# Where the operands of the main matrix products lie in SBUF, modulo 256 bytes

## The chip, the cores and the metric

The kernel runs on one core of a Trainium2 chip. The metric is the device time of one execution in microseconds; the time before is the median of three runs. TensorE (PE) multiplies, VectorE (DVE) and ScalarE (ACT) work element by element, GpSimd (POOL) and SyncE (SP) mostly start transfers here. SBUF is the on-chip memory from which all of them read: 128 partitions, each a row of bytes, and an address below is a byte address within a partition.

## What is computed

One layer of a decoder trunk on 288 tokens (256 of a prompt, 32 of eight short samples), in float32. A short convolution mixer and a gated delta-rule mixer share one input projection; their outputs are merged, and a feed-forward block follows:

```python
proj = x @ w_in                                   # 2048 -> 11280 columns
y_a = (gB * conv_out) @ w_a_out
y_b = o.reshape(Bsz, L, D_GDN).astype(x.dtype) @ w_b_out
merged = sigmoid(m_a) * y_a + sigmoid(m_b) * y_b
x = layer_norm(ALPHA * x + merged @ w_o, ln1_g, ln1_b)
hid = square(relu(x @ w_up))                      # 2048 -> 8192
x = layer_norm(ALPHA * x + hid @ w_down, ln2_g, ln2_b)
```

## The kernel before

**Tiling.** Every large product is computed transposed: the features of the result lie on the partitions and the 288 tokens run along the row. A block of weights is four slices of 128 input rows by 256 output columns (512 KB), and a group of blocks makes 256 columns of the result in two banks of PSUM. The table `blocks` lists all of them in the order in which they run: the input projection with the delta rule woven between its matmuls, the merge (sigmoid gates from `w_in`, each with its product with `w_a_out` or `w_b_out`), the product with `w_o`, and four times a quarter of `w_up` (eight groups) followed by a quarter of `w_down` (eight groups; the last of them has its final group turned round, L747).

**High and low parts.** Float32 precision is put together from three products of a rounded type. Each operand is split into a high part, rounded by ScalarE (`split_hi`, L184), and a low part, the remainder, made by VectorE (`split_lo`, L139 as its helper). For every slice k of 128 rows and both halves of 128 columns, `matmuls` issues the three products high x high, high weights x low activations, and low weights x high activations, so six matmuls to a slice, in this order: xh with the first half of `hi`, xl with the same half, xh and xl with the second half, then xh with the first half of `lo` and with its second half. In the profile these are lines L216 (with `hi`) and L218 (with `lo`). Each matmul has its own load of 128 x 128 weights.

**Names.** The activations are `xh` and `xl` in the projection and for the gates, `ahl` and `ohl` (high and low halves in one tile) for the products with `w_a_out` and `w_b_out`, `mh` and `ml` for `w_o`, `dh` and `dl` for `w_up`, and `hh` and `hl` for `w_down`. `hh` and `hl` take over the memory of `xh` and `xl` (the pool's tags XH and XL), and the others share four regions, R1 to R4. A tag names one piece of memory which several tiles use in turn.

**Loads and lead.** `load` starts the transfer of a block seven blocks ahead, and the two splits follow three blocks ahead of the matmuls, in four buffers each for `raw`, `hi` and `lo`. The order of instructions on each engine is written out by hand; no scheduler moves anything. What places the tiles in memory is the order in which pools and tags are first asked for, and their sizes.

**Places.** A row of `hi` or `lo` is 1024 bytes to a slice and 512 to a half, so all weights of one kind lie at one place modulo 256. One slice of activations is 288 tokens, 1152 bytes (four and a half times 256), so that the places of successive slices alternate by 128. `dh` and `dl` hold 290 columns a slice (NX, with two columns for the layer norm's gain and offset, which only the first quarter of `w_up` uses), 1160 bytes, so their place moves on by 136 with each slice; `ohl` has this pitch too. `w_o`'s evacuation `wo_evac` writes `dh` and `dl` for the first quarter, and `normal` overwrites them, 288 columns wide, for the other three. `acc` is the running sum of the feed-forward block.

The lines that walk through the activations:

```python
for k in range(kb):
    xh_, xl_ = ah[:, k0 + k, 0:n], al[:, k0 + k, 0:n]
    ...
    for o, c, x in both[::2] + both[1::2] if i == 0 else both:
        pe.matmul(o, h[:, k, c], x, start=st and x is xh_, stop=False)
    for o, c in ts:
        pe.matmul(o, l[:, k, c], xh_, start=False, stop=en)
```

Of the kernel before, what the change touches and what calls it, by code (L numbers as in the profile page):

```python
# [9 lines left out]
F32 = mybir.dt.float32  # L10
# [6 lines left out]
P = 128  # L17
# [4 lines left out]
NX = NT + 2  # L22
# [79 lines left out]
def hybrid_kernel(ctx: ExitStack, tc: tile.TileContext, A):  # L102
# [141 lines left out]
    ones = cst("ones")  # L244

    xh = xp.tile([P, KT, NT], F32R, tag="XH", name="xh")
    xl = xp.tile([P, KT, NT], F32R, tag="XL", name="xl")
    hw = cp.tile([P, 24, 28], F32, name="hw")
    hwa = cp.tile([P, 8, 19], F32, name="hwa")
# [155 lines left out]
    def yb_evac(p):  # L405
        def f(ps):
            if p == 0:
                ph["mh"] = ph["pool"].tile([P, KT, NT], F32R, tag="R1", name="mh")
                ph["ml"] = ph["pool"].tile([P, KT, NT], F32R, tag="R2", name="ml")
            s = slice(2 * p, 2 * p + 2)  # L410
            t = ph["pool"].tile([P, 2, NT], F32, tag="yt", name=nm("yt"), bufs=2)
            tt(t, ps[:, :, 0:NT], ph["sg"], MUL)
            tt(t, t, ph["mg"][:, s, :], ADD)
            act.copy(ph["mh"][:, s, :], t)
            tt(ph["ml"][:, s, :], t, ph["mh"][:, s, :], SUB)
        return [f]
# [4 lines left out]
    for p in range(8):  # L421
        add_group(w_in, C_MB + GW * p, 0, KT, acts_x, [sig_evac])
        add_group(A["w_b_out"][0], GW * p, 0, 8, lambda: (ph["oh"], ph["ol"]), yb_evac(p))

    def wo_evac(p):
        q = slice(2 * p, 2 * p + 2)

        def resid(ps):
            pl = ph["pool"]
            if p == 0:  # L430
                ph["dl"] = pl.tile([P, KT, NX], F32R, tag="R3", name="dl")
                ph["dh"] = pl.tile([P, KT, NX], F32R, tag="R4", name="dh")
                t = ap_.tile([P, 2, H, NT], F32, tag="ao", name="lns").rearrange("p a h t -> p (a h) t")
                ph["qa"], ph["da"], ph["c"] = t[:, 0:2], t[:, 2:4], t[:, 4]
                ph["ln"] = [t[:, 5 + u] for u in range(4)]
                dh, dl = ph["dh"], ph["dl"]
                gbc = lnp[:, 0:32].rearrange("p (a k) -> p k a", a=2)
                act.copy(hmr, ones)
                act.copy(dh[:, :, NT:NX], gbc)
                tt(dl[:, :, NT:NX], gbc, dh[:, :, NT:NX], SUB)  # L440
            ph["s"] = pl.tile([P, 2, NT], F32, tag="yt", name=nm("s"), bufs=2)
            dd = ph["s"]
            stt(dd, xh[:, q, :], ALPHA, ps[:, :, 0:NT], MUL, ADD)
            stt(dd, xl[:, q, :], ALPHA, dd, MUL, ADD)
            if p:
                tt(dd, dd, bmid(ph["c"], 2), SUB)

        def centre(ps):
            tt(ph["c"], ph["s"][:, 0, :], ph["s"][:, 1, :], ADD)
            ph["chl"] = high_low(ph["c"], "sg")  # L450

        def shift(ps):
            cps = gtile()
            dd = ph["s"]
            row_sums(cps[:, 0:NT], ph["chl"])
            act.mul(ph["c"], cps[:, 0:NT], 1.0 / 256)
            tt(dd, dd, bmid(ph["c"], 2), SUB)

        def scaled(ps):
            dd, qa, da = ph["s"], ph["qa"], ph["da"]  # L460
            sd = ph["pool"].tile([P, 2, NT], F32, tag="sg", name=nm("sd"), bufs=2)
            for u in range(2):
                k = 2 * p + u
                dve.tensor_scalar(out=sd[:, u, :], in0=dd[:, u, :], scalar1=lnp[:, k:k + 1], scalar2=None, op0=MUL)
            act.copy(ph["dh"][:, q, 0:NT], sd)
            tt(ph["dl"][:, q, 0:NT], sd, ph["dh"][:, q, 0:NT], SUB)

        def sums(ps):
            dd, qa, da = ph["s"], ph["qa"], ph["da"]
            if p == 0:  # L470
                act.activation(qa, dd, AF.Square)
                act.copy(da, dd)
            else:
                s2 = ph["pool"].tile([P, 2, NT], F32, tag="sg", name=nm("sq"), bufs=2)
                act.activation(s2, dd, AF.Square)
                tt(da, da, dd, ADD)
                tt(qa, qa, s2, ADD)

        def both(*fs):
            def f(ps):  # L480
                for g in fs:
                    g(ps)
            return f

        if p == 0:
            return [resid, centre, lambda ps: None, shift, both(scaled, sums)]
        if p < 7:
            return [resid, both(scaled, sums)]
        return [both(resid, scaled, sums), halve, lambda ps: None, lambda ps: None, norms]
# [17 lines left out]
    def norms(ps):  # L507
        s1, s2 = gtile(), gtile()
        for t, u in ((s1, "dahl"), (s2, "qahl")):
            row_sums(t[:, 0:NT], ph[u])  # L510
        dm, va, av, nb = ph["ln"]
        act.mul(dm, s1[:, 0:NT], INV_D)
        tt(va, dm, dm, MUL)
        stt(va, s2[:, 0:NT], INV_D, va, MUL, SUB)
        act.activation(va, va, AF.Sqrt, bias=epsc[:, 0:1])
        dve.reciprocal(out=av, in_=va)
        stt(nb, dm, -1.0, av, MUL, MUL)
        ph["acc"] = ph["pool"].tile([P, KT, NT], F32, tag="R1", name="acc")


    def normal(p):
# [18 lines left out]
            act.mul(ph["acc"][:, q, :], t, ALPHA)  # L540

        def f3():
            t, h = tl["t"], ph["dh"][:, q, 0:NT]
            act.copy(h, t)
            tt(ph["dl"][:, q, 0:NT], t, h, SUB)
        return f, f2, f3

    for p in range(8):
# [317 lines left out]
    mark["up"] = len(blocks)  # L866
    for c in range(4):
        for p in range(8):
            add_group(A["w_up"][0], 2048 * c + GW * p, 0, KT, lambda: (ph["dh"], ph["dl"]), up_evac(c, p),
                      NT if c else NX)  # L870
        mark["down", c] = len(blocks)
        if c == 3:
            mark["down3"] = len(blocks)
        acts_h = lambda: (ph["hh"], ph["hl"])
        for p in range(8 if c < 3 else 7):
            add_group(A["w_down"][0], GW * p, 2048 * c, KT, acts_h, down_evac(c, p))
# [755 lines left out]
    steps = x_steps(0, 1)  # L1632
    t0, o0 = steps[0]()
    his[0] = wp.tile([P, KB, GW], F32R, tag="hi", name=nm("hi"))
    los[0] = wp.tile([P, KB, GW], F32R, tag="lo", name=nm("lo"))
    t, h0, l0 = raw.pop(0), his[0], los[0]

# [45 lines left out]
    for i in range(len(blocks)):  # L1683
# [50 lines left out]
        if i == mark["merge"]:  # L1734
            gcm.__exit__(None, None, None)
            p3 = pool("p3")
            ph["pool"] = p3
            r1 = p3.tile([P, KT, NT], F32R, tag="R1", name="ahl")
            r4 = p3.tile([P, KT, NX], F32R, tag="R4", name="ohl")
            ph["mg"] = p3.tile([P, KT, NX], F32, tag="R3", name="mg")[:, :, 0:NT]  # L1740

            def halves(key, r, src):
                for q in range(2):
                    s = slice(4 * q, 4 * q + 4)
                    s8 = slice(8 + 4 * q, 12 + 4 * q)
                    act.copy(r[:, s, 0:NT], src[:, s, :])
                    tt(r[:, s8, 0:NT], src[:, s, :], r[:, s, 0:NT], SUB)
                ph[key + "h"], ph[key + "l"] = r[:, 0:8, :], r[:, 8:16, :]

            halves("a", r1, gd["ao"][:, 0])  # L1750
            at(i + 9, lambda: halves("o", r4, gd["ao"][:, 1]))
# [58 lines left out]
```

## Time and profile before

| what | value |
|---|---|
| median of 3 runs (lowest to highest) | 1650.71 us (1650.47 to 1650.87) |
| span of the profiled execution | 1648.8 us |
| matmuls of TensorE, all | 12857 |
| of these, three-product matmuls 288 or 290 columns wide (L216, L218) | 11808 |
| busy PE, DVE, ACT, POOL | 1641.3, 986.9, 780.0, 137.0 us |

The span runs from the first to the last instruction, and the device time holds some 2 us more. PE's busy time is no measure of how well it runs, since matmuls are pipelined and their ends are modelled. What can be read is how far apart the starts of successive matmuls stand, or, in a long stretch without a wait, its length over the number of matmuls in it.

The ends of the stages, as the times at which the first matmul on new activations starts: merge 424.07 us, `w_o` 717.39 us, the quarters of `w_up` 819.64, 1024.83, 1229.04 and 1433.25 us, those of `w_down` 922.86, 1127.07, 1331.28 and 1535.49 us, the last group 1627.45 us.

### The profile page before, as it was taken

What the parts mean: (1) busy time and instruction counts of PE and PEld (TensorE: products, weight loads), DVE (VectorE), ACT (ScalarE), POOL (GpSimd) and SP (SyncE); (2) the same over time, 40 slices, a digit from 0 to 9 for tenths busy, and PEclk for the clock granted to TensorE, in tenths of its full rate; (3) what the DMA queues carried; (4) which work ended last, traced back from release to release, by engine and by line L of the source; (5) the groups of instructions that cost most, each with busy time, mean ns of one, the idle gap of its engine ahead of it and who ended that gap; (6) DMA issues with size and microseconds to landing.
All of it is one profiled execution on the core that took longest, in us unless ns stands there. A gap on an engine that the chain in (4) does not pass through costs nothing.

```text
span 1648.8 us, 30931 instructions
## 1 busy us (share of the span) xinstructions
PE 1641.3 (100%) x12857; PEld 1628.9 (99%) x12857; DVE 986.9 (60%) x1342; ACT 780.0 (47%) x1215; POOL 137.0 (8%) x286
## 2 busy tenths in 40 slices
PE   9999999999999999999999999999999999999998
PEld 8999999999999999999999999999999999999998
DVE  6787788878544444457776666444444444444466
ACT  7774678367533333334354454443334433344454
POOL 1232214234000000000000000000000000000111
PEclk9999999999999999999999999999999999999999
DMA  8567466846655555555565555555555555555652
GB/s 267 176 174 207 141 173 198 226 116 187 189 167 166 166 166 167 167 167 160 177 202 166 167 166 167 166 165 165 165 164 164 165 166 166 167 166 167 181 164 100
DMA packets 278999, 282.49 MB, mean 171 GB/s; under 512 B 15075, under 2 KB 272920, under 8 KB 278596
## 3 DMA queue, kind: packets, MB, share of 16 engines
q1 hardware_dynamic: 274394, 268.42, 54.7%
q0 software_dynamic: 4032, 11.63, 2.5%
q8 instruction: 101, 1.65, 0.4%
q10 hardware_dynamic: 432, 0.46, 0.1%
q14 instruction: 40, 0.33, 0.1%
HBM read 272.83 MB, written 7.63 MB: 170 GB/s over the span
## 4 chain that ended last, share of the span: by engine, by line
PE 98%; ACT 0%; DVE 0%; POOL 0%; issue 0%; ACTq 0%
PE acc L216 63%; PE acc L218 31%; PE acc L747 1%; PE g L1538 0%; PE g L1558 0%; PE g L1561 0%; PE g L1338 0%; PE g L1238 0%; PE g L1511 0%; PE g L1550 0%; PE g L1347 0%; PE g L1042 0%; PE g L701 0%; PE g L1422 0%; PE g L1399 0%; DVE lo L139 0%
## 5 line engine op out<-in xcount | busy, mean ns | idle before, releaser
L139 DVE TENSOR_TENSOR lo<-raw,hi 128x1024 fp32r<-128x1024 f32 (+1 forms) x503 | 606.7, 1210 | 560.0 <-ACT hi L184 558.5
L184 ACT CAST hi<-raw 128x1024 fp32r<-128x1024 f32 (+1 forms) x499 | 518.8, 1042 | 724.9 <-PE acc L216 630.2
L216 PE MATMUL acc<-xh,hi 128*128 128x288 f32 x1408 | 397.3, 298 | 1.0 <-ACT xh L956 1.0
L216 PE MATMUL acc<-xl,hi 128*128 128x288 f32 x1408 | 393.8, 295 | 0.0
L218 PE MATMUL acc<-xh,lo 128*128 128x288 f32 x1408 | 302.0, 295 | 0.1
L216 PE MATMUL acc<-dl,hi 128*128 128x288 f32 (+1 forms) x1024 | 287.7, 295 | 0.0
L216 PE MATMUL acc<-dh,hi 128*128 128x288 f32 (+1 forms) x1024 | 287.4, 295 | 0.0
L216 PE MATMUL acc<-hl,hi 128*128 128x288 f32 x992 | 277.8, 295 | 0.0
L216 PE MATMUL acc<-hh,hi 128*128 128x288 f32 x992 | 277.4, 294 | 0.0
L216 PEld LDWEIGHTS acc<-xh,hi 128*128 128x128 f32 x1408 | 264.3, 188 | 3.4 <-ACT xh L956 1.5
L216 PEld LDWEIGHTS acc<-xl,hi 128*128 128x128 f32 x1408 | 264.2, 188 | 0.6
L218 PEld LDWEIGHTS acc<-xh,lo 128*128 128x128 f32 x1408 | 225.9, 188 | 0.4 <-DVE lo L139 0.3
L218 PE MATMUL acc<-dh,lo 128*128 128x288 f32 (+1 forms) x1024 | 219.8, 296 | 0.0
L218 PE MATMUL acc<-hh,lo 128*128 128x288 f32 x992 | 213.2, 296 | 0.0
L216 PEld LDWEIGHTS acc<-dh,hi 128*128 128x128 f32 x1024 | 193.3, 189 | 0.0
L216 PEld LDWEIGHTS acc<-dl,hi 128*128 128x128 f32 x1024 | 192.8, 188 | 0.0
L216 PEld LDWEIGHTS acc<-hh,hi 128*128 128x128 f32 x992 | 186.4, 188 | 0.4 <-issue 0.4
L216 PEld LDWEIGHTS acc<-hl,hi 128*128 128x128 f32 x992 | 186.1, 188 | 0.0
L218 PEld LDWEIGHTS acc<-dh,lo 128*128 128x128 f32 x1024 | 164.6, 188 | 0.0
L218 PEld LDWEIGHTS acc<-hh,lo 128*128 128x128 f32 x992 | 159.0, 188 | 0.0
L216 PE MATMUL acc<-mh,hi 128*128 128x288 f32 x256 | 71.9, 297 | 0.0
L216 PE MATMUL acc<-ml,hi 128*128 128x288 f32 x256 | 71.7, 295 | 0.0
(424 smaller groups left out, 1475.0 us busy)
## 6 DMA issues: line engine op xcount, KB each, us to landing
raw<-in_w_in_dram SPq DMA_DIRECT2D x175, 512.0 KB, 3.8
raw<-in_w_up_dram SPq DMA_DIRECT2D x128, 512.0 KB, 3.8
raw<-in_w_down_dram SPq DMA_DIRECT2D x128, 512.0 KB, 3.6
raw<-in_w_o_dram SPq DMA_DIRECT2D x32, 512.0 KB, 3.5
raw<-in_w_a_out_dram SPq DMA_DIRECT2D x16, 512.0 KB, 3.7
raw<-in_w_b_out_dram SPq DMA_DIRECT2D x16, 512.0 KB, 3.5
out_dram<-S POOLq DMA_DIRECT2D x8, 512.0 KB, 4.5
S<-in_state_gdn_dram POOLq DMA_DIRECT2D x4, 512.0 KB, 6.4
```

Of the source, the lines that this page charges most:

```text
L139: dve.tensor_tensor(out=out, in0=a, in1=b, op=op)
L184: act.copy(his[i][:, k:k + step], raw[i][:, k:k + step])
L216: pe.matmul(o, h[:, k, c], x, start=st and x is xh_, stop=False)
L218: pe.matmul(o, l[:, k, c], xh_, start=False, stop=en)
L747: pe.matmul(out, x[:, kk, c], w[:, k, :], start=False, stop=stop)
```

## The change

No instruction is added, removed or moved on any engine, and the waits between the engines stay as they were. What changes is where the operands lie:

- A gap of 64 bytes between the buffers of `hi` and those of `lo`, and one of 128 bytes between `xh` and `xl`. Neither is ever written.
- The region R1, too, is now 16 x 290 columns long like R3 and R4 (18560 bytes, an odd multiple of 128), so that the regions behind it shift.
- `dh` and `dl` are read with a pitch of 1160 bytes by the first quarter of `w_up` alone. For the other three, `normal` writes the same memory with a pitch of 1152 (`nh`, `nl`).
- `mh`, `acc`, and the halves in `ahl` and `ohl` have a pitch of 1152; the low half begins 128 bytes behind the end of the high one.

The places modulo 256, counted from the high weights:

| operand | before, even and odd slices | after, even and odd slices |
|---|---|---|
| `hi` | 0 | 0 |
| `lo` | 0 | 64 |
| `xh`, `hh` | 0, 128 | 64, 192 |
| `xl`, `hl` | 0, 128 | 192, 64 |
| `mh` | 0, 128 | 192, 64 |
| `ml` | 0, 128 | 64, 192 |
| `ahl`, high half | 0, 128 | 192, 64 |
| `ahl`, low half | 0, 128 | 64, 192 |
| `ohl`, high half | 0, then 136 more with each slice | 64, 192 |
| `ohl`, low half | 64, then 136 more | 192, 64 |
| `dh`, first quarter of `w_up` | 0, then 136 more | 64, then 136 more |
| `dl`, first quarter | 128, then 136 more | 192, then 136 more |
| `dh`, other quarters | 0, then 136 more | 64, 192 |
| `dl`, other quarters | 128, then 136 more | 192, 64 |

```diff
     xh = xp.tile([P, KT, NT], F32R, tag="XH", name="xh")
+    xp.tile([P, 32], F32, tag="gap", name="xgap")
     xl = xp.tile([P, KT, NT], F32R, tag="XL", name="xl")
...
-                ph["mh"] = ph["pool"].tile([P, KT, NT], F32R, tag="R1", name="mh")
+                ph["mh"] = rows(ph["pool"].tile([P, KT * NX], F32R, tag="R1", name="mh"))
...
+    def rows(t):
+        return t[:, 0:KT * NT].rearrange("p (k t) -> p k t", t=NT)
...
-                ph["dl"] = pl.tile([P, KT, NX], F32R, tag="R3", name="dl")
-                ph["dh"] = pl.tile([P, KT, NX], F32R, tag="R4", name="dh")
+                for u, tag in (("l", "R3"), ("h", "R4")):
+                    t = pl.tile([P, KT * NX], F32R, tag=tag, name="d" + u)
+                    ph["d" + u], ph["n" + u] = t.rearrange("p (k t) -> p k t", t=NX), rows(t)
...
-        ph["acc"] = ph["pool"].tile([P, KT, NT], F32, tag="R1", name="acc")
+        ph["acc"] = rows(ph["pool"].tile([P, KT * NX], F32, tag="R1", name="acc"))
...
-            t, h = tl["t"], ph["dh"][:, q, 0:NT]
+            t, h = tl["t"], ph["nh"][:, q, :]
             act.copy(h, t)
-            tt(ph["dl"][:, q, 0:NT], t, h, SUB)
+            tt(ph["nl"][:, q, :], t, h, SUB)
...
-            add_group(A["w_up"][0], 2048 * c + GW * p, 0, KT, lambda: (ph["dh"], ph["dl"]), up_evac(c, p),
+            add_group(A["w_up"][0], 2048 * c + GW * p, 0, KT, lambda c=c: (ph["nh"], ph["nl"]) if c else (ph["dh"], ph["dl"]), up_evac(c, p),
                       NT if c else NX)
...
     his[0] = wp.tile([P, KB, GW], F32R, tag="hi", name=nm("hi"))
+    wp.tile([P, 16], F32, tag="gap", name="wgap", bufs=1)
     los[0] = wp.tile([P, KB, GW], F32R, tag="lo", name=nm("lo"))
...
-            r1 = p3.tile([P, KT, NT], F32R, tag="R1", name="ahl")
-            r4 = p3.tile([P, KT, NX], F32R, tag="R4", name="ohl")
+            r1 = p3.tile([P, KT * NX], F32R, tag="R1", name="ahl")
+            r4 = p3.tile([P, KT * NX], F32R, tag="R4", name="ohl")
...
             def halves(key, r, src):
+                n, o = 8 * NT, 8 * NT + 32
+                hi, lo = (r[:, u:u + n].rearrange("p (k t) -> p k t", t=NT) for u in (0, o))
                 for q in range(2):
                     s = slice(4 * q, 4 * q + 4)
-                    s8 = slice(8 + 4 * q, 12 + 4 * q)
-                    act.copy(r[:, s, 0:NT], src[:, s, :])
-                    tt(r[:, s8, 0:NT], src[:, s, :], r[:, s, 0:NT], SUB)
-                ph[key + "h"], ph[key + "l"] = r[:, 0:8, :], r[:, 8:16, :]
+                    act.copy(hi[:, s, :], src[:, s, :])
+                    tt(lo[:, s, :], src[:, s, :], hi[:, s, :], SUB)
+                ph[key + "h"], ph[key + "l"] = hi, lo
```

## The prediction

> **What bounds the kernel now.** I begin with the page: the span, each engine's share, and the chain of work that ended last.
>
> ```profile
> span 1648.8 us, 30931 instructions
> PE 1641.3 (100%) x12857; PEld 1628.9 (99%) x12857; DVE 986.9 (60%) x1342; ACT 780.0 (47%) x1215; POOL 137.0 (8%) x286
> PE 98%; ACT 0%; DVE 0%; POOL 0%; issue 0%; ACTq 0%
> ```
>
> TensorE is the chain, and 98% says that hardly anything else is on it. Is there a wait within it that could go? The view of who waited for whom, for PE alone, has four rows in all:
>
> ```profile
> PE acc L216 <- ACT xh L956: 1.0, 1, 1.0
> PE g L894 <- DVE warm L889: 1.0, 1, 1.0
> PE g L809 <- ACT g L806: 0.3, 1, 0.3
> PE g L805 <- DVE R L139: 0.2, 1, 0.2
> ```
>
> That is 2.5 us (columns: total, times, longest), at the start and in the tail. In the main products no matmul waits for data, so the time is the number of matmuls times the distance between their starts. The busy times in the page don't give that distance (a matmul of 288 columns is shown as 295 ns long, and they overlap). The busy time by stretches does: each of the stretches below is one stage, the ones of 102 us hold 768 three-product matmuls, the first holds the merge with 2208.
>
> ```profile
> 424.07:717.39 293.32, 293.32 (x2210) 293.32 (x2209) 135.83 (x123) 112.98 (x119) 0.00 (x0) 1.00 0.57 168
> 819.64:922.86 103.22, 103.22 (x774) 103.22 (x773) 69.81 (x83) 47.67 (x68) 1.64 (x3) 1.00 0.60 187
> 922.86:1024.83 101.97, 101.97 (x770) 101.97 (x769) 69.85 (x83) 52.42 (x68) 0.00 (x0) 1.00 0.54 166
> 1024.83:1127.07 102.24, 102.24 (x770) 102.24 (x769) 49.92 (x48) 41.99 (x48) 0.00 (x0) 1.00 0.55 165
> 1127.07:1229.04 101.97, 101.97 (x770) 101.97 (x769) 45.20 (x41) 34.83 (x35) 0.00 (x0) 1.00 0.55 166
> 1229.04:1331.28 102.24, 102.24 (x770) 102.24 (x769) 49.25 (x47) 41.41 (x47) 0.00 (x0) 1.00 0.54 165
> ...
> 1433.25:1535.49 102.24, 102.24 (x770) 102.24 (x769) 49.25 (x47) 41.40 (x47) 2.00 (x4) 1.00 0.55 168
> ```
>
> The columns after the length are busy time and count of PE, weight loads, DVE, ACT and POOL, then the granted clock and the transfers. (Counts are two too high, because matmuls reach over the ends.) A quarter of w_down takes 101.97 us, 132.77 ns a matmul; a quarter of w_up with 288 columns 102.24 us, 133.13 ns; the merge 293.32 / 2208 = 132.85 ns. The clock is 1.00 in each. Two things matter here. The first and the second w_down quarter agree to 0.01 us though VectorE worked 69.85 us beside one and 45.20 beside the other: neighbours don't set this rate. And w_up differs from w_down by 0.27 us in the same number of matmuls of the same size; of what the matmuls ask for, what differs is the pitch of the activations, 1160 bytes against 1152. So places in memory do show in the rate, by 0.3% here. The 11808 three-product matmuls at 132.8 ns are 1568 of the 1648.8 us: 0.1 ns on each is 1.2 us.
>
> How much of a matmul's distance could places govern at all? The longest pieces of the chain hold some matmuls of 256 columns:
>
> ```profile
> 1629.87 4.31 PE acc L747 x36
> ```
>
> 4.31 / 36 = 119.7 ns. Against 132.8 ns for 288 columns that is 13.1 ns for 32 columns, 0.41 ns a column; 288 columns are then 118 ns, and 14.8 ns of every distance are something else. A start-up cost and a collision of the two reads (activations streaming, next weights loading) would both look like this.
>
> **Finer: slice by slice.** The timeline of PE in the first w_down quarter, rows of the two low-weight matmuls alone; each begins 0.27 us before the end of its slice, so successive starts stand one slice, six matmuls, apart. The first row is slice 2 of its group.
>
> ```profile
> start us, us, engine line op out<-in xcount [idle before <-releaser]
> 924.98 0.43 PE L218 MATMUL acc<-hh,lo 128*128 128x288 f32 x2
> ...
> 925.78 0.43 PE L218 MATMUL acc<-hh,lo 128*128 128x288 f32 x2
> ...
> 926.57 0.43 PE L218 MATMUL acc<-hh,lo 128*128 128x288 f32 x2
> ...
> 927.38 0.43 PE L218 MATMUL acc<-hh,lo 128*128 128x288 f32 x2
> ...
> 928.17 0.43 PE L218 MATMUL acc<-hh,lo 128*128 128x288 f32 x2
> ...
> 928.97 0.43 PE L218 MATMUL acc<-hh,lo 128*128 128x288 f32 x2
> ...
> 929.76 0.43 PE L218 MATMUL acc<-hh,lo 128*128 128x288 f32 x2
> ```
>
> The steps are 0.80, 0.79, 0.81, 0.79, 0.80, 0.79. The three that end in an odd slice sum to 2.41 us, 133.9 ns a matmul; the three that end in an even one to 2.37 us, 131.7 ns. In an even slice activations and weights lie at the same place modulo 256, in an odd one 128 bytes apart. Now the same rows of the w_up quarter that begins at 1024.83 us, where the place moves by 136 from slice to slice:
>
> ```profile
> 1026.97 0.43 PE L218 MATMUL acc<-dh,lo 128*128 128x288 f32 x2
> ...
> 1030.95 0.44 PE L218 MATMUL acc<-dh,lo 128*128 128x288 f32 x2
> ...
> 1031.76 0.43 PE L218 MATMUL acc<-dh,lo 128*128 128x288 f32 x2
> ...
> 1035.77 0.43 PE L218 MATMUL acc<-dh,lo 128*128 128x288 f32 x2
> ...
> 1036.56 0.42 PE L218 MATMUL acc<-dh,lo 128*128 128x288 f32 x2
> ...
> 1037.35 0.43 PE L218 MATMUL acc<-dh,lo 128*128 128x288 f32 x2
> ...
> 1038.14 0.43 PE L218 MATMUL acc<-dh,lo 128*128 128x288 f32 x2
> ...
> 1039.75 0.43 PE L218 MATMUL acc<-dh,lo 128*128 128x288 f32 x2
> ```
>
> From slice 2 (1026.97) to slice 2 of the next group (1039.75) are 12.78 us, 133.1 ns a matmul over sixteen different places. Single slices read 0.81 us (1030.95 to 1031.76, 135.0 ns) or 0.79 (the three from 1035.77 to 1038.14, 131.7 ns). So sixteen distances between activations and weights all give 131 to 135 ns, and their mean is within 0.3% of what two distances give. I read this as one rate with a small part that depends on place and largely averages out.
>
> **The change part by part.**
>
> *Instructions.* None is added or removed, no wait is added, and no queue's order moves, so neither SP nor POOL has anything new before a transfer. `raw` stays where it was. The two gap tiles are never touched. Some writes by ACT and DVE (to `nh`, `nl`, the halves of `ahl` and `ohl`) now run over one contiguous stretch; they could become cheaper or dearer by a little, but DVE idles half of each w_up quarter (49.25 of 102.24 us busy), works three blocks ahead, and PE waits for it nowhere in these stages: 0 us. If that cover were gone, one split (L139) of 1.21 us a block would be at stake:
>
> ```profile
> L139 DVE TENSOR_TENSOR lo<-raw,hi 128x1024 fp32r<-128x1024 f32 (+1 forms) x503 | 606.7, 1210 | 560.0 <-ACT hi L184 558.5
> ```
>
> *Pitch of 1152 in three quarters of w_up.* If they take the rate of w_down: 3 x (102.24 - 101.97) = 0.81 us less. `ohl`, 384 matmuls, loses the same 0.36 ns each: 0.14 us. Sum 0.95 us. The first quarter (103.22 us, 290 columns) keeps its pitch: 0.
>
> *Places of all 11808.* Before, activations lay 0 or 128 bytes from whichever weights were loading, outside the stages with the pitch of 1160. After, they lie 64 or 192 from `hi` (four of six matmuls load `hi` next) and 0 or 128 from `lo`. The trace doesn't show this layout. From both sides: if all went at the fast 131.7 ns of the even slices, 11808 x (132.77 - 131.67) = 13.0 us less; if all went at the slow 133.9 of the odd ones, 11808 x (133.89 - 132.77) = 13.2 us more. Single slices go further: all at 135.0 ns would be 26.3 us more, and a slice of 0.79 us, shown to 10 ns, may be 130.0 ns, 33 us less; that all slices do so is not to be expected. The nearest row is the mean of sixteen distances, 133.1 ns, and the pitch accounts for its excess over 132.8: I take **0**.
>
> *Sum.* Against the profiled execution: 1648.8 - 0.95 = 1647.9 us of span. The median of the runs, 1650.71 us, is 1.9 us above the span, and the same 1.9 us stay: 1649.8 us.
>
> A rule speaks for nothing at all here. The Trainium skill (TensorE: Matmul & The Clock Gate, Part 2) says that TensorE has two independent read ports into SBUF, so that loading the next weights takes no bandwidth from the running matmul; by it the relative places are worth 0 and only the pitch's 0.95 us could remain. The trace doesn't quite agree: the 0.79 and 0.81 us of neighbouring slices have the same instructions and differ in places.
>
> **The rivals.**
>
> *The places fall well (faster).* What an odd slice pays is a meeting of the two reads at a distance of 128, and 64 or 192 avoid it as 0 does. For it: the steps of 0.80 and 0.79 alternate as regularly as the places do. It decides if the distance to `hi` counts, since four loads of six have it. All matmuls at 131.7 ns and the pitch: 1650.71 - 13.0 - 0.95 = 1636.8 us.
>
> *The places fall badly (slower).* The new distances behave as 128 does, or worse, in even slices too. For it: slice 8 of the w_up quarter is the only one of the old layout whose high products have the new even places (`dh` at 64, `dl` at 192 from `hi`), and the step that ends in it is the 0.81 us from 1030.95 to 1031.76. Against it: that step includes two matmuls of slice 7, and its neighbours read 0.80 as well. All at 133.9 ns: 1650.71 + 13.2 - 0.95 = 1663.0 us. It wins from the point at which the mean of even and odd slices rises above 133.1 ns, 0.28 ns more than now.
>
> *The reads part altogether.* If all of the 14.8 ns beyond the columns were collisions and the new places ended them, 11808 x 14.8 = 175 us would go, 1475 us. Sixteen distances, none of which comes below 130 ns, speak against it. Beside it: the Trainium skill (same page, Back-to-back issue gap) gives 288 / 2.4 + 2.5 = 122.5 ns, an estimate from its formula, by which some 122 us could be had; no run here shows such a distance.
>
> **How the numbers follow.** A measurement of this kernel can tell about 0.2%, 3.3 us, from no change. Forecast, the places average out: 0.37. Places fall well: 0.33. Places fall badly: 0.28. Reads part: 0.02. Around the forecast lies a scatter of some 2 us, so that of its 0.37 I count 0.28 as same, 0.06 as faster, 0.03 as slower. That makes faster 0.41, same 0.28, slower 0.31. The likeliest single case gives 1649.8 us. The range must reach over both middle rivals and part of the single slices' extremes: 1626 (some 25 us less, three quarters of the way to 130.0 ns) to 1667 us (17 us more, two thirds of the way to 135.0 ns); the likeliest case alone has 1646 to 1653.
>
> **What would show it.** In the changed profile the busy time by stretches is the test: w_down quarters at 101.97 us and w_up quarters 2 to 4 at 101.97 instead of 102.24 mean that the forecast holds with its pitch term; w_up down and w_down unchanged is the pitch alone; both at 101.1 or at 102.8 are the two rivals. The timeline's steps by slice should still alternate or vary by 0.01 to 0.02 us; if all read alike, the places did count. The first quarter of w_up, whose pitch stays, moves only if the distance to the weights matters or `lo` does. Waits of PE should stay at 2.5 us; a new one behind DVE or ACT in the merge or w_up would make the cover wrong. I am wrong in the main point if the distance of a matmul leaves 132.4 to 133.1 ns.

## The result, and the profile after

| | before | after |
|---|---|---|
| median of four runs (lowest to highest) | 1650.79 us (1650.47 to 1650.92) | 1632.45 us (1632.24 to 1632.61) |
| span of the profiled execution | 1648.8 us | 1630.6 us |

The ratio is 0.9889, with an interval of 0.9875 to 0.9903: 18.3 us less. That lies inside the range, but the forecast, 1649.8 us, is 17.3 us off. Of the cases, "the places fall well" came nearest, and even its 1636.8 us was 4.4 us too long.

The page of the changed kernel, the same three lines as before:

```profile
span 1630.6 us, 30931 instructions
...
PE 1623.6 (100%) x12857; PEld 1610.9 (99%) x12857; DVE 987.2 (61%) x1342; ACT 779.7 (48%) x1215; POOL 139.5 (9%) x286
...
PE 92%; DVE 2%; ACT 2%; DMA 1%; issue 1%; POOL 0%; DVEq 0%; ACTq 0%
```

As many instructions as before, and VectorE and ScalarE busy as long as before (986.9 and 780.0 us then). The chain now names DVE, ACT and DMA, which it hardly did. That alone looks like new waits. The view of who waited for whom, PE alone (total us, times, longest), says otherwise; these are all its rows:

```profile
PE g L899 <- DVE warm L894: 1.0, 1, 1.0
PE acc L216 <- ACT xh L961: 0.5, 1, 0.5
PE g L814 <- ACT g L811: 0.3, 1, 0.3
PE g L810 <- DVE R L139: 0.2, 1, 0.2
PE acc L218 <- DVE lo L139: 0.2, 1, 0.2
```

They sum to 2.2 us, where it was 2.5. One of them (L218 behind `lo`) is new, 0.2 us long, and stands at 28 us, in the start of the kernel. The chain changes engines elsewhere: at 320.10 us, in the projection, it goes over to VectorE and follows splits and transfers back to 232.39 us. PE was busy through that stretch all the same (after the length: PE, clock, transfers):

```profile
232.39:320.10 87.71, 87.62 (x685) 1.00 0.72 204
```

So the chain is a different tie, not a different bound.

The busy time by stretches, each row a stage as in the prediction (after the length: PE, weight loads, DVE, ACT, POOL, then clock and transfers). The first row is the merge, the second `w_o`, the third the first quarter of `w_up` (290 columns), then quarters of `w_down` and `w_up` in turn:

```profile
420.07:709.89 289.82, 289.82 (x2211) 289.82 (x2209) 137.92 (x125) 112.95 (x120) 0.00 (x0) 1.00 0.58 171
709.89:810.88 100.99, 100.99 (x773) 100.99 (x771) 73.61 (x92) 43.81 (x53) 0.00 (x0) 1.00 0.54 165
810.88:914.44 103.56, 103.56 (x774) 103.56 (x773) 69.90 (x83) 47.65 (x68) 1.64 (x3) 1.00 0.59 186
914.44:1015.13 100.69, 100.69 (x770) 100.69 (x769) 69.81 (x83) 52.29 (x68) 0.00 (x0) 1.00 0.55 168
1015.13:1115.83 100.70, 100.70 (x771) 100.70 (x769) 49.90 (x48) 42.01 (x48) 0.00 (x0) 1.00 0.55 168
1115.83:1216.52 100.69, 100.69 (x770) 100.69 (x769) 45.21 (x41) 34.74 (x35) 0.00 (x0) 1.00 0.55 168
1216.52:1317.21 100.69, 100.69 (x770) 100.69 (x769) 49.23 (x47) 41.42 (x47) 0.00 (x0) 1.00 0.56 168
```

The clock stayed at 1.00. Stage by stage against before: up to the merge 420.07 for 424.07 us, the merge 289.82 for 293.32, `w_o` 100.99 for 102.25, the first quarter of `w_up` 103.56 for 103.22, three quarters of `w_up` 100.69 or 100.70 for 102.24, three of `w_down` 100.69 or 100.70 for 101.97, and 112.00 us from the last quarter's start to the end for 113.31. That is -4.00 - 3.50 - 1.26 + 0.34 - 3 x 1.55 - 3 x 1.28 - 1.31 = -18.2 us, the whole difference of the spans. It is spread over every stage with 288 columns. A `w_down` quarter has 100.69 / 768 = 131.11 ns from matmul to matmul, where it was 132.77; the stages gained 1.4 (projection) to 2.0 ns (`w_up`) on a matmul. Only the stage with 290 columns did not gain.

The timeline of PE in the first `w_down` quarter, the same rows (low weights, one slice apart) as in the prediction:

```profile
916.54 0.42 PE L218 MATMUL acc<-hh,lo 128*128 128x288 f32 x2
...
917.33 0.42 PE L218 MATMUL acc<-hh,lo 128*128 128x288 f32 x2
...
918.12 0.42 PE L218 MATMUL acc<-hh,lo 128*128 128x288 f32 x2
...
918.90 0.42 PE L218 MATMUL acc<-hh,lo 128*128 128x288 f32 x2
...
919.69 0.42 PE L218 MATMUL acc<-hh,lo 128*128 128x288 f32 x2
...
922.84 0.42 PE L218 MATMUL acc<-hh,lo 128*128 128x288 f32 x2
```

The steps are 0.79, 0.79, 0.78, 0.79, and (922.84 - 916.54) / 8 = 0.7875 us on the mean of eight. They look alike, but only because the view shows 10 ns. The trace keeps starts to 1 ns, and there the steps of this quarter still alternate: 783 ns into an odd slice and 790 into an even one, where the quarter before had 802 and 791. So the even slices kept their length, and the odd ones fell by 19 ns, below the even ones.

### The profile page after: what moved, and what is told of

Read it like the earlier page. It is cut to its first block, busy times and chain, and to the rows that moved or that the text cites. A ratio compares the mean times of both kernels' runs of the same rounds, so it can differ in the third digit from the quotient of the medians.

```text
span 1630.6 us, 30931 instructions
## 1 busy us (share of the span) xinstructions
PE 1623.6 (100%) x12857; PEld 1610.9 (99%) x12857; DVE 987.2 (61%) x1342; ACT 779.7 (48%) x1215; POOL 139.5 (9%) x286
## 4 chain that ended last, share of the span: by engine, by line
PE 92%; DVE 2%; ACT 2%; DMA 1%; issue 1%; POOL 0%; DVEq 0%; ACTq 0%
PE acc L216 60%; PE acc L218 29%; DMA raw<-in_w_in_dram 1%; DVE lo L139 1%; PE acc L752 1%; ACT hi L184 1%; PE g L1543 0%; PE g L1563 0%; PE g L1566 0%; PE g L1343 0%; PE g L1516 0%; PE g L1555 0%; ACT ao L1605 0%; ACT b L1587 0%; PE g L1352 0%
## 5 line engine op out<-in xcount | busy, mean ns | idle before, releaser
L218 PE MATMUL acc<-xh,lo 128*128 128x288 f32 x1408 | 298.2, 293 | 0.2 <-DVE lo L139 0.2
L218 PEld LDWEIGHTS acc<-xh,lo 128*128 128x128 f32 x1408 | 226.2, 188 | 0.4 <-DVE lo L139 0.4
L218 PE MATMUL acc<-dh,lo 128*128 128x288 f32 (+1 forms) x1024 | 217.0, 293 | 0.0
L218 PE MATMUL acc<-hh,lo 128*128 128x288 f32 x992 | 209.1, 292 | 0.0
L218 PEld LDWEIGHTS acc<-dh,lo 128*128 128x128 f32 x1024 | 164.6, 188 | 0.0
L218 PEld LDWEIGHTS acc<-hh,lo 128*128 128x128 f32 x992 | 159.2, 188 | 0.0
```

## Experiments

The first question was whether the places themselves did it, and which of them (theory D: the distances between activations and weights; theory X: the distance between high and low activations alone), or whether moving the tiles only changed how the reads and writes of VectorE, ScalarE and the transfers meet TensorE's (theory N, neighbours). Later theories are explained in the expectations that name them. Each experiment is a single execution, except e6 with ten; the kernel before ran between 1650.16 and 1652.18 us in thirteen executions beside e6 to e8. Below, a layout is written (lo; xh, xl): the places modulo 256 behind the high weights in even slices. With a pitch of 1152, odd slices have the activations 128 further. Before was (0; 0, 0), the change is (64; 64, 192) or (64; 192, 64).

### e1_places: the matmuls alone, 64 layouts

A kernel of its own: four tiles, the six matmuls of a slice in the kernel's order, 16 slices to a layout, one layout behind the other, nothing else running.

```python
CONFIGS = [(0, l, a, b, 1152) for l in (0, 64, 128, 192) for a in (0, 64, 128, 192) for b in (0, 64, 128, 192)]
...
            for t in range(2):
                for u, m in enumerate((x(xh, a0), x(xl, b0))):
                    pe.matmul(acc[:, t, 0:n], wt(hi, h0, t), m, start=(k == 0 and u == 0), stop=False)
            for t in range(2):
                pe.matmul(acc[:, t, 0:n], wt(lo, l0, t), x(xh, a0), start=False, stop=(k == slices - 1))
```

> Only matmuls are left: 64 groups of 16 slices x 6 matmuls of 288 columns with the same order of high and low products, a pitch of 1152 bytes, and nothing else running. Each group has one of the 64 placements: low weights, high activations and low activations at 0, 64, 128 or 192 bytes from the high weights (low weights change slowest, low activations fastest). The rest of the layer is left out. Theory D (the distance between the activations that stream and the weights that load decides): the placement 0, 0, 0 takes 132.8 ns a matmul as in the old w_down quarters, the placement 64, 64, 192 takes 131.1 ns as in the new ones, and low weights at 0 against 64 make a difference of a few tenths. Theory X (only the places of the activations to each other matter, the weights don't): the time depends on the distance of low to high activations alone, 131.1 ns for all 16 placements with 128 between them, 132.8 ns for the 16 with 0, whatever the low weights are. Theory N (the other engines' accesses to memory take part): with the others idle all 64 placements run alike, faster than 131.1 ns.

The busy time by stretches, one layout of 96 matmuls to a row (PE, weight loads, ACT, POOL, clock, transfers). In order: (64; 0, 192), (64; 64, 0), (64; 64, 64), the change's (64; 64, 192) and (64; 192, 64), then (128; 0, 128), (128; 128, 0) and (0; 64, 192).

```profile
296.18:308.98 12.80, 12.80 (x98) 12.80 (x97) 0.00 (x0) 0.00 (x0) 1.00 0.01 1
308.98:321.77 12.79, 12.79 (x99) 12.79 (x98) 0.00 (x0) 0.00 (x0) 1.00 0.01 1
321.77:334.46 12.69, 12.69 (x98) 12.69 (x97) 0.00 (x0) 0.00 (x0) 1.00 0.00 0
347.15:359.74 12.59, 12.59 (x99) 12.59 (x98) 0.00 (x0) 0.00 (x0) 1.00 0.00 1
423.04:435.63 12.59, 12.59 (x99) 12.59 (x98) 0.00 (x0) 0.00 (x0) 1.00 0.00 0
486.41:499.17 12.76, 12.76 (x99) 12.76 (x98) 0.00 (x0) 0.00 (x0) 1.00 0.01 1
562.65:575.19 12.54, 12.54 (x98) 12.54 (x97) 0.00 (x0) 0.00 (x0) 1.00 0.01 1
143.88:156.56 12.68, 12.68 (x98) 12.68 (x97) 0.00 (x0) 0.00 (x0) 1.00 0.00 1
```

The change's layout takes 12.59 / 96 = 131.1 ns with every other engine idle, exactly what the full kernel shows. The old one takes 132.8 here too (row under e4). So N falls: the places alone do it. X falls as well, since the low weights count: (0; 64, 192) takes 12.68 / 96 = 132.1 ns and (64; 64, 192) 131.1. Over all 64, the distance from xh to xl shifts the mean by less than 1% (132.2, 132.0, 131.7 and 132.5 ns for distances of 0, 64, 128 and 192, from the fifth slice of each layout on), while one distance holds layouts from fast to slow: 128 apart are (64; 64, 192) at 131.1 and (128; 0, 128) at 12.76 / 96 = 132.9. D is right that the distances to the weights count, but a fixed price for each distance doesn't explain the oddest pair: (128; 0, 128) and (128; 128, 0), at 132.9 and 12.54 / 96 = 130.6 ns. With slices alternating by 128 these are the same endless sequence of places, begun one slice apart.

And the lengths come in steps: 12.54, 12.59, 12.69, 12.80 differ by multiples of 0.053 us, which is 6.67 ns for two slices. By the starts of single matmuls about four pairs of slices in five lie within 1 ns of a whole multiple of 6.67 ns. The rows in between differ: (128; 0, 128), 12.76, begins with two longer pairs and then runs at 1593.3 ns a pair (132.8 ns a matmul), a whole multiple; (0; 64, 192), 12.68, repeats three pairs of 1588, 1584 and 1581 ns.

### e2_pitch: the pitch without the places

The new pitch of 1152 everywhere, with all gaps taken out and the regions lengthened to a multiple of 256, so that every operand lies at 0 or 128 as before.

```diff
-    xp.tile([P, 32], F32, tag="gap", name="xgap")
...
-                ph["mh"] = rows(ph["pool"].tile([P, KT * NX], F32R, tag="R1", name="mh"))
+                ph["mh"] = rows(ph["pool"].tile([P, KT * NX + 32], F32R, tag="R1", name="mh"))
...
-    wp.tile([P, 16], F32, tag="gap", name="wgap", bufs=1)
...
-                n, o = 8 * NT, 8 * NT + 32
+                n, o = 8 * NT, 8 * NT
```

> The pitch of 1152 alone: w_up quarters 2 to 4 and the second half of the merge have it, while all activations lie 0 or 128 bytes from high and low weights, as w_down had it before. Theory D and the prediction's pitch term: w_up quarters 2 to 4 at 101.97 us instead of 102.24, w_down at 101.97, total 1 us under the kernel before, 1649.8. Theory P (the pitch is what brought the 18 us): 1632 us, all stages. In the first quarter of w_up, which keeps 1160, high and low activations now lie at one place instead of 128 apart: theory X expects it to move, theory D too, but by less than 1 us.

1650.36 us, beside 1650.29 for the kernel before. The stretches of the first `w_up` quarter, the first `w_down` quarter and the second `w_up` quarter:

```profile
819.83:923.41 103.58, 103.58 (x774) 103.58 (x773) 69.81 (x83) 47.62 (x68) 1.64 (x3) 1.00 0.59 186
923.41:1025.38 101.97, 101.97 (x770) 101.97 (x769) 69.85 (x83) 52.40 (x68) 0.00 (x0) 1.00 0.54 166
1025.38:1127.36 101.98, 101.98 (x771) 101.98 (x770) 49.92 (x48) 42.03 (x48) 0.00 (x0) 1.00 0.55 166
```

So the theory that the pitch brought the 18 us (P) falls. `w_up` falls from 102.24 to 101.98 us in three quarters, about 0.8 us in all, as the prediction's pitch term said. But the first quarter rises from 103.22 to 103.58: its pitch is the old one, yet `dh` and `dl` now lie at one place instead of 128 bytes apart. With 0.19 us more ahead of it (819.83 for 819.64), nothing is left: the pitch without the change's places is worth -0.2 us of span (1648.6 for 1648.8).

### e3_lo0: the change without its gap at the low weights

```diff
-    wp.tile([P, 16], F32, tag="gap", name="wgap", bufs=1)
     los[0] = wp.tile([P, KB, GW], F32R, tag="lo", name=nm("lo"))
+    wp.tile([P, 16], F32, tag="gap", name="wgap", bufs=1)
```

> The changed kernel with the low weights back at the place of the high ones, activations as changed (64 and 192 from both). Theory D: two of six matmuls load low weights, at distances 64 and 192 instead of 0 and 128, so each slice pair changes by a few ns: 1629 to 1640 us. Theory X: no change, 1632.5 us. If the low weights' 64 bytes are what the gain hangs on, it goes back to about 1650 us.

1641.34 us, 8.9 more than the changed kernel. The first `w_down` quarter and the second of `w_up`:

```profile
918.76:1020.16 101.40, 101.40 (x770) 101.40 (x769) 69.84 (x83) 52.35 (x68) 0.00 (x0) 1.00 0.55 167
1020.16:1121.57 101.41, 101.41 (x771) 101.41 (x769) 49.91 (x48) 42.02 (x48) 0.00 (x0) 1.00 0.55 167
```

101.40 / 768 = 132.03 ns; e1 has 12.68 / 96 = 132.1 for (0; 64, 192). Without the gap at the low weights, which two matmuls of six use, about half of the gain is lost. X expected no change and falls; D expected 1629 to 1640 us, a little less than this. The table of e1 predicts the full kernel here, neighbours and all.

### e4_grid: columns, common shifts, and places that don't alternate

The kernel of e1 with two groups for each entry: the old and the new layout at 17 numbers of columns; both moved as a whole; finer distances; and a pitch of 1280 (five times 256), with which every slice lies at the same place.

```python
CONFIGS = [p + (1152, n) for n in (256, 272, 280, 282, 284, 286, 288, 290, 292, 294, 296, 304, 320, 352, 384, 448, 512)
           for p in (OLD, NEW)]
CONFIGS += [tuple(v + s for v in p) + (1152, 288) for s in (16, 32, 48, 64, 128, 192) for p in (OLD, NEW)]
...
CONFIGS += [(0, l, a, b, 1280, 288) for l in (0, 64, 128, 192) for a in (0, 64, 128, 192) for b in (0, 64, 128, 192)]
```

> Matmuls alone again, the rest of the layer is left out; each placement runs two groups of 16 slices. Theory G (time goes by a grid: two slices, after which the places repeat, always last a whole number of steps of 6.67 ns, and a placement gains or loses whole steps): widths from 280 to 296 columns in steps of 2 (12 x 0.83 = 10.0 ns per two slices) move the length of two slices by 6.67 or 13.33 ns, never by 10.0; a pitch of 1280, where every slice lies at one place, gives single slices of whole steps. Theory L (each matmul has a price by its places, added up): every 2 columns add 10.0 ns per two slices, the same at both placements. Theory R (only distances count): shifting all four operands by 16 to 192 bytes leaves 132.8 and 131.1 ns as they are. Theory W (what lies beyond the columns' own time arises while weights load, which takes as long for every width): the excess over 0.417 ns a column stays 12 to 15 ns from 256 to 512 columns; against it, theory S (each column costs a little more): the excess doubles from 256 to 512.

Stretches of 192 matmuls each: new with 286 columns; old, new with 288; old, new with 290; old with 292. Behind them, with the pitch of 1280: (64; 64, 192) for 192 matmuls, then 96 each of (0; 0, 0), (0; 128, 128), (64; 64, 192) once more, and (64; 192, 64).

```profile
327.13:352.53 25.40, 25.40 (x194) 25.40 (x193) 0.00 (x0) 0.00 (x0) 1.00 0.01 1
352.53:378.02 25.49, 25.49 (x194) 25.49 (x193) 0.00 (x0) 0.00 (x0) 1.00 0.00 1
378.02:403.19 25.17, 25.17 (x194) 25.17 (x193) 0.00 (x0) 0.00 (x0) 1.00 0.01 1
403.19:429.12 25.93, 25.93 (x195) 25.93 (x193) 0.00 (x0) 0.00 (x0) 1.00 0.00 1
429.12:455.03 25.91, 25.91 (x194) 25.91 (x193) 0.00 (x0) 0.00 (x0) 1.00 0.01 1
455.03:480.84 25.81, 25.81 (x195) 25.81 (x193) 0.00 (x0) 0.00 (x0) 1.00 0.00 1
...
2109.47:2134.75 25.28, 25.28 (x194) 25.28 (x193) 0.00 (x0) 0.00 (x0) 1.00 0.00 1
2134.75:2147.39 12.64, 12.64 (x98) 12.64 (x97) 0.00 (x0) 0.00 (x0) 1.00 0.01 1
2261.77:2274.57 12.80, 12.80 (x98) 12.80 (x97) 0.00 (x0) 0.00 (x0) 1.00 0.00 1
2426.94:2439.70 12.76, 12.76 (x98) 12.76 (x97) 0.00 (x0) 0.00 (x0) 1.00 0.00 1
2503.29:2516.07 12.78, 12.78 (x98) 12.78 (x97) 0.00 (x0) 0.00 (x0) 1.00 0.00 0
```

In ns for one matmul, by columns, from the starts of the matmuls (with the old layout and 256 columns from the second group alone, as the first waits for its data):

| columns | 256 | 280 | 284 | 286 | 288 | 290 | 292 | 512 |
|---|---|---|---|---|---|---|---|---|
| old | 118.3 | 127.9 | 131.7 | 130.8 | 132.8 | 135.0 | 134.4 | 230.7 |
| new | 117.8 | 128.9 | 130.6 | 132.3 | 131.1 | 135.0 | 134.5 | 231.1 |

Three things follow. First, the length isn't a smooth function of the columns: 290 cost more than 292, with the new layout 286 more than 288, and at 280 and at 512 columns the new layout is the slower one. So "every 2 columns add 10.0 ns" (L in the expectation) falls. The steps (G) hold in part. Two slices still mostly last a whole number of 6.67 ns, but not always (the old layout with 286 columns: 1570 ns, half a step off), and they don't move by one or two steps from width to width as G expected: from 282 to 284 columns the old layout doesn't move at all. Nor does either view of the columns fit. From 118.3 ns at 256 columns, the expectation's 0.417 ns a column on top of a fixed part (W) would give 225.1 ns at 512, and a time in proportion to the columns (S) 236.7; the old layout takes 230.7, halfway.

Second, moving all four operands by 32, 64, 128 or 192 bytes changes nothing (132.8 and 131.1 to 131.2 ns each time), by 16 or 48 a little (132.2 and 131.9). So what counts is how the operands lie to each other (R), but only for moves by these multiples of 32. The other distances in steps of 16 bytes and the pitches of 1168, 1184 and 1216 gave 131.2 to 133.4 ns, none below the change.

Third, a slice has no price of its own. At one constant place the new layout's two kinds of slices take 12.76 / 96 = 132.9 and 12.78 / 96 = 133.1 ns here, and alternating they take 131.1. And the first kind, (64; 64, 192) at a pitch of 1280, ran twice: the same places take 25.28 / 192 = 131.7 ns in one part of this run and 132.9 in another. What ran before must count too. For the old layout prices would nearly have added up: 12.64 / 96 = 131.7 and 12.80 / 96 = 133.3 ns alone, 132.8 in turn.

### e5_search: odd multiples of 32 bytes

The kernel of e1 with 192 further layouts, to look for one in which the collisions end.

```diff
-CONFIGS = [(0, l, a, b, 1152) for l in (0, 64, 128, 192) for a in (0, 64, 128, 192) for b in (0, 64, 128, 192)]
+CONFIGS = [(0, l, a, b, 1152) for l in (0, 64, 128, 192) for a in range(0, 256, 32) for b in range(0, 256, 32)
+           if a % 64 or b % 64]
```

> Matmuls alone, 192 placements in which at least one of the activations stands at an odd multiple of 32 bytes. Theory G: all lengths of two slices are whole steps, most between 1576.7 and 1600 ns (131.4 to 133.3 ns a matmul), mean about 132.2 ns as in the 64 placements before, so the old layout (132.8) is on the slow side of its kind and the new one (131.1) near the fast end, with few below it. If collisions could be avoided altogether by a finer offset, some placement would fall clearly out of this band, to 125 ns or less.

A miss as a search. Stretches of (0; 0, 96), (0; 128, 224) and of a fast one, (0; 192, 160):

```profile
70.02:82.95 12.93, 12.93 (x98) 12.93 (x97) 0.00 (x0) 0.00 (x0) 1.00 0.56 163
401.36:414.31 12.95, 12.95 (x99) 12.95 (x98) 0.00 (x0) 0.00 (x0) 1.00 0.01 1
541.67:554.28 12.61, 12.61 (x99) 12.61 (x98) 0.00 (x0) 0.00 (x0) 1.00 0.01 1
```

The lengths run from 131.4 to 12.95 / 96 = 134.9 ns, 132.7 on the mean. No layout breaks away from the rest; the change's 131.1 is already near the fast end. The two slowest, (0; 0, 96) and (0; 128, 224), are the same sequence begun one slice apart, and slow from either start.

### e6_best: the fastest layout of the table in the full layer

(128; 128, 0), 12.54 / 96 = 130.6 ns in e1, put into the changed kernel: a gap of 128 bytes at the low weights, and xl (with `hl`) in a pool of its own.

```diff
-    xp.tile([P, 32], F32, tag="gap", name="xgap")
-    xl = xp.tile([P, KT, NT], F32R, tag="XL", name="xl")
+    xl = xlp.tile([P, KT, NT], F32R, tag="XL", name="xl")
...
-    wp.tile([P, 16], F32, tag="gap", name="wgap", bufs=1)
+    wp.tile([P, 32], F32, tag="gap", name="wgap", bufs=1)
```

> The whole layer with the fastest placement of the first table of 64: low weights 128 bytes behind the high ones, high activations at 128 and 0 in even and odd slices, low activations at 0 and 128 (w_up and the second half of the merge: the same with even and odd slices exchanged). Theory G (whole steps, and the same pair of slices can settle at different lengths by what ran before): quarters of w_down and the projection at 1566.7 ns per two slices, 100.27 us a quarter, where they settle as (128, 128, 0) did in the table; w_up at 100.27 or, settled as (128, 0, 128) did, at 101.97 us. The total is then between 1626 us (all fast) and 1637 us (the stages with the exchanged order slow). Theory L (a price for each pair of places, added up): both orders hold the same pairs, so all stages run alike, at one rate between 130.7 and 132.9 ns.

1649.13 us (1648.36 to 1650.55), 0.9989 of before, interval 0.998 to 0.9999. A miss. The first `w_down` quarter and the second of `w_up`, from the slowest of the ten executions:

```profile
923.66:1025.63 101.97, 101.97 (x770) 101.97 (x769) 69.84 (x83) 52.32 (x68) 0.00 (x0) 1.00 0.54 166
1025.63:1127.62 101.99, 101.99 (x771) 101.99 (x770) 49.90 (x48) 41.98 (x48) 0.00 (x0) 1.00 0.55 166
```

101.97 / 768 = 132.8 ns, not 130.6: neither G's 1626 to 1637 us nor its split between the stages came in. This is the layout whose sequence had two lengths in e1. The full kernel settled on the longer one and stayed there through whole stages. That isn't one fixed rate either (L), since the projection shows both lengths. Two stretches of 25 slices each:

```profile
250.46:270.05 19.59, 19.59 (x152) 19.59 (x151) 17.73 (x27) 17.14 (x43) 13.28 (x16) 1.00 0.75 220
281.12:301.04 19.92, 19.92 (x153) 19.92 (x151) 17.76 (x34) 10.04 (x16) 4.94 (x11) 1.00 0.64 179
```

19.59 / 150 = 130.6 ns and 19.92 / 150 = 132.8 ns, with the same activations, and the weights at the same places modulo 256. Between them other matmuls interrupt the run (from 270.83 us). So the miss isn't that the tiles lie otherwise in the full kernel than in e1. A short time in a table is a possibility, not a promise.

### e7_same_x: the change without its gap between xh and xl

```diff
-    xp.tile([P, 32], F32, tag="gap", name="xgap")
     xl = xp.tile([P, KT, NT], F32R, tag="XL", name="xl")
+    xp.tile([P, 32], F32, tag="gap", name="xgap")
```

> The changed kernel with the gap of 128 bytes behind xl instead of in front of it, so that high and low activations of the projection and of w_down lie at one place (64, 192); all other tiles stay as changed. The table of 64 has 132.2 ns for it: w_down quarters 1904 / 1.2 x 64 = 101.55 us instead of 100.69, w_up unchanged at 100.69, the total about 1632.5 + 3 x 0.86 + 0.77 (last quarter) + 1.0 ns x 4224 (projection and gates) = 1640 us. If the distance of the activations to each other didn't matter, all stages would stay and the total with them, 1632.5 us.

1640.45 us, 8.0 more than the changed kernel. The first `w_down` quarter, which uses these places, and the second of `w_up`, which doesn't:

```profile
919.04:1020.59 101.55, 101.55 (x771) 101.55 (x770) 69.85 (x83) 52.43 (x68) 0.00 (x0) 1.00 0.54 166
1020.59:1121.29 100.70, 100.70 (x770) 100.70 (x769) 49.89 (x48) 41.99 (x48) 0.00 (x0) 1.00 0.56 168
```

101.55 / 768 = 132.2 ns, as (64; 64, 64) in e1 (12.69 / 96 = 132.2), and the total is that of the expectation. `w_up` keeps its 100.70 us. The stage that was moved lost, the one beside it did not.

### e8_slow: a layout from the slow end

The kernel of e2 with 96 bytes between xh and xl: (0; 0, 96), e5's slow sequence, in the projection and `w_down`. The products of the other regions lie at 96 and 224 by it.

```diff
     xh = xp.tile([P, KT, NT], F32R, tag="XH", name="xh")
+    xp.tile([P, 24], F32, tag="gap", name="xgap")
     xl = xp.tile([P, KT, NT], F32R, tag="XL", name="xl")
```

> A layout that should be slower than either: everything as in the run with the pitch alone, but the low activations of the projection and of w_down 96 bytes from the high ones (0 and 128 against 96 and 224, low weights at 0). The search has 1944 steps of 0.83 ns per two slices for it, 135.0 ns a matmul: w_down quarters 103.68 us. w_up then has both activations at 96 and 224: 132.5 ns, 101.76 us. In all about 1650.3 + 2.2 ns x 7200 (projection, gates, w_down) = 1666 us. If only multiples of 64 or the gap as such counted, it would stay near 1650.

1662.15 us, 11.5 more than before. The first `w_down` quarter and the second of `w_up`:

```profile
929.54:1033.17 103.63, 103.63 (x770) 103.63 (x769) 69.85 (x83) 52.27 (x68) 0.00 (x0) 1.00 0.53 163
1033.17:1134.93 101.76, 101.76 (x770) 101.76 (x769) 49.89 (x48) 41.91 (x48) 0.00 (x0) 1.00 0.55 166
```

Both stages take what the tables said, 134.9 and 132.5 ns a matmul. The tables are thus good for slowing down as well as for speeding up; the whole came out 4 us under its expectation.

## Why the prediction was right in its range and wrong in its main term, step by step

**The range: right, by its width.** 1632.45 us lies inside 1626 to 1667 because the range reached towards single slices of 130.0 ns, at which the prediction didn't expect all slices to run. That it held is luck as far as the mechanism goes.

**What bounds the kernel: right.** The time is the number of matmuls times their distance, and neighbours don't set it. e1 has the full kernel's 132.8 and 131.1 ns with the other engines idle.

**Instructions, 0 us: right.** PE's waits are 2.2 us for 2.5, DVE's busy time 987.2 us for 986.9.

**Pitch, -0.95 us: right where it was worked out, wrong in what was left out.** Three quarters of `w_up` fall by about 0.26 us each in e2, as said. That this is the pitch alone isn't shown: by the table of places, high and low activations of `w_up` also lay 128 bytes apart where those of `w_down` lay at one place, and e2 changes both. "The first quarter keeps its pitch: 0" was wrong: +0.36 us in e2 and +0.34 in the changed kernel. In e2 its `dh` and `dl` lost their distance of 128 bytes; in the changed kernel they kept it and moved by 64 towards `hi`, and I had put the quarter under "pitch" alone. Net -0.2 us of span instead of -0.95.

**"Places of all 11808: I take 0": the step that failed.** Taking off e2's -0.2 us, the places carry -18.0 of -18.2 us. By the rates it is (11808 - 768) x (132.77 - 131.11) = 18.3 us less, the 768 being the first `w_up` quarter, which e2 and the changed kernel run alike. The size of the error is 1.66 ns on a matmul. My argument was that sixteen distances in `w_up` average 133.1 ns, close to what two distances average, so that any new layout must land there. Two things were wrong in it. The mean over a moving place says nothing of a layout that repeats every two slices: e1 shows such layouts from 130.6 to 133.3 ns, most of them in steps of 6.67 ns per two slices. The change shifted the sequence by three steps, 20 ns in some 1593, or 1.25%: in `w_down` 242 of 246 pairs of slices last 239 steps before, and 245 of 246 last 236 after, each to the nearest step. And I looked for the price of a slice at its place. e4 shows that slices have none: two kinds at 132.9 and 133.1 ns alone run at 131.1 in turn, and one of them took 131.7 ns elsewhere in the same run. The single slices of the timeline (0.79, 0.81 us) could then not bound the new layout from below, and the bound of -13.0 us, all slices at the old even slices' rate, was passed by 5 us: the odd slices fell below that rate (783 ns against 791).

The Trainium skill (TensorE: Matmul & The Clock Gate, Part 2) would make the places worth 0, as I weighed it. The measurements decide against that reading: the same matmuls with nothing beside them take 130.6 to 134.9 ns by the places alone. They don't say that the ports are the cause.

**"The places fall well": right in sign, wrong in its mechanism.** A meeting of the reads at a distance of 128 that 64 and 192 avoid would let any layout with these distances gain. e3 keeps xh and xl at 64 and 192 from the high weights and loses half of the gain (0.71 of 1.28 us in a `w_down` quarter) through `lo` alone. e7 keeps `hh` at 64 and 192 and `lo` at 64, has `hl` there too, and loses two thirds (0.86 of 1.28 us). The whole gain needs both gaps together: either one alone keeps only a part.

**"The places fall badly" and "the reads part".** Bad layouts exist, as e8 shows with 103.63 us a stage; the change isn't one. All layouts tried with 288 columns lie between 130.6 and 134.9 ns, a band of some 3%; none comes near the 118 ns that this case needs, so no run shows any of its 175 us. Whether other places would isn't shown.

**The signs I named.** The rate spoke: 131.1 ns is outside the 132.4 to 133.1 ns that I had given as the limit of being right. "If all read alike, the places did count" was no good sign, since a view in steps of 10 ns can't tell steps of 783 and 790 ns apart: they look alike, and are not.

**Left open.** Where the step of 6.67 ns comes from; what decides on which of its lengths a sequence settles (that the same places can settle on two is shown in e1, e4 and e6, and that what ran before decides is suggested by it, not shown further); whether the two reads collide at all; why 290 columns take more than 292. Other orders of the six matmuls in a slice, which also change the sequence, weren't tried. No kernel tried was faster than the changed one.

## What to carry to other kernels

In this kernel, a long and nearly unbroken run of equal matmuls, the relative places of the streamed operand and of the weights being loaded were worth about 1% either way, and an average over other places didn't tell what a given layout does. Measure layouts in a kernel of matmuls alone, in the real order, columns and pitch, and then confirm in the full kernel: most table values carried over to 0.1%, one did not. Change one gap at a time, and re-measure when the columns change, since the faster layout changes with them (at 280 and 512 columns it is the old one). Another order of the matmuls wasn't tried and should be measured too. And read a view only to the digits that it has.

## What the runs showed of the hardware that I had not expected

- The length of a repeating pair of slices mostly comes in steps of 6.67 ns (groups of 12.54, 12.59, 12.64, 12.69 us, 0.053 apart), so that a shift of 64 bytes often costs or brings whole steps at once.
- The same places can settle on two lengths: one sequence took 130.6 or 132.9 ns a matmul in e1, begun one slice apart, and 130.6 and then 132.8 within the projection of e6; another, with a pitch of 1280, took 131.7 and 132.9 in e4.
- More columns can take less time: 134.4 ns for 292 against 135.0 for 290 in the old layout, 131.1 for 288 against 132.3 for 286 in the new one.
- Moving everything together by 32, 64, 128 or 192 bytes changes nothing, by 16 or 48 it does (132.8 to 132.2 ns in the old layout, 131.1 to 131.9 in the new one).
